# One product per head and direction for the next state and the outputs of an RWKV-7 scan, with the block columns of every second head reversed

## The chip, the cores and the metric

The kernel runs on one core of a Trainium2 chip. The metric is the device time of one execution in microseconds (us); lower is better. The kernel before took 3946.70, 3950.52 and 3961.48 us in three runs, median 3950.52 us.

## What is computed

Two layers of a diffusion backbone on 512 latent and 256 context tokens of 1024 channels in fp32. A layer is a feed-forward, a token mixing, and a second feed-forward. The mixing projects the tokens once, gives half of the channels to a neighbourhood attention and the other half to RWKV-7, a recurrence over tokens that is run forward and backward, and projects both back. Of the recurrence (eight heads of 64 channels) the reference says, per head and direction:

```python
def rwkv_scan(state0, r, decay, k, v, kk, a, reverse):
    emit = r is not None

    def step(S, inp):
        r_t, w_t, k_t, v_t, kk_t, a_t = inp
        removal = jnp.einsum('bhvk,bhk->bhv', S, kk_t)
        S = (S * w_t[:, :, None, :]
             - removal[..., None] * (kk_t * a_t)[:, :, None, :]
             + v_t[..., None] * k_t[:, :, None, :])
        out = jnp.einsum('bhvk,bhk->bhv', S, r_t) if emit else None
        return S, out
```

The context is scanned first, then the latent tokens. In the second (last) layer the context's outputs are not wanted, so `r` is None there.

## The kernel before

Everything is one program; a static scheduler sets the order of the instructions on each engine, and each engine then runs its own list in that order.

**The feed-forwards** (`up`, line 364, and `product`, line 322) are long runs of matrix products with weights split into a high and a low part; they take most of the span and the change does not touch them.

**The mixing** (`mix`, line 1096) issues seven kinds of steps side by side through `drive` (line 71), which hands out the next ready step by weights of TensorE time: the scan (`chains`), the blocks' inverses (`solves`), the blocks (`all_blocks`), the projections, the attention, the modulation of the next layer, and the output projection (`outs`). The scan has the first rank.

**The scan.** The 768 tokens of a direction are cut into 24 chunks of 32. Four heads (two pairs) form a group and are scanned together in both directions, so a chunk has eight head-and-direction products, and there are 2 layers x 2 groups x 24 = 96 chunks. `rwkv_block` (line 780) and `rwkv_solves` (line 746) prepare, for each head, direction and chunk, a block of 128 rows and 128 columns in a tile named `st`. Its columns are `B_S` (64: the next state), `B_O` (32: the outputs), `B_U` (32: U, the removal term of the chunk's tokens). Head e = 0 of a pair keeps the state in rows 0 to 63 and V and U in rows 64 to 127; head e = 1 has it the other way round (`SR`, `VR`, `UR`, line 44).

`rwkv_chain` (line 914) then does, per chunk, on a state tile x (the profile calls it `k`):

- eight products into 32 rows each that give U (line 938), into bank `ch`; ACT copies head 0's part and DVE (line 940) head 1's part back into x;
- eight products into 64 rows each for the next state (line 944), the two heads of a pair in different halves of the rows, into the other half of bank `ch`; ACT and DVE (line 946) copy it into the next state tile;
- where outputs are wanted (80 of the 96 chunks), eight products into 32 rows each (line 950), all into the same 32 rows `QUADS[c]` of bank `co`. After four chunks (a unit) one ACT copy of the whole bank writes the tile `ob`.

After certain units `rwkv_read` (line 987) reads `ob`: a product `pj` (line 996), a chain of small DVE, POOL and ACT steps, transposes (line 1013) and a product `pg` (line 1020). The output projection of these heads follows it.

An fp32 product appears in the trace as two MATMUL records and two LDWEIGHTS records, so eight products are 16 records. "Tile shape" below means the rows and columns of TensorE's array that a product uses, read from the weights' shape: 128\*32, 128\*64, 128\*128 and so on.

Of the kernel before, what the change touches and what calls it, by code (L numbers as in the profile page):

```python
# [12 lines left out]
ALU = mybir.AluOpType  # L13
# [10 lines left out]
# half of the columns of the feed-forward's first product, even as the products ask for  # L24
# [4 lines left out]
# head pairs are scanned two at a time  # L29
# [77 lines left out]
class Net:  # L107
# [62 lines left out]
    def mod(self, l, i, tag, cols, bank):  # L170
# [3 lines left out]
        for c0 in range(0, KD * D, step):  # L174
# [6 lines left out]
            # the four column groups at once  # L181
# [71 lines left out]
    def prep_wino(self, kt, tag="g3"):  # L253
        """The right operands of k-tiles kt and kt + 4: x scaled, and twice the shifts."""
# [51 lines left out]
    def weight(self, src):  # L306
        """The parts of four tiles of weights: (high, low)."""
# [6 lines left out]
    def product(self, w, xh, xl, segs, banks="g"):  # L314
        """The product's segments one after the other: (columns, PSUM) as each is finished."""
# [25 lines left out]
    def up(self, raw, ctx, hh, hl):  # L341
        """A tile of the hidden features."""
# [80 lines left out]
    def accumulate(self, src, k0, n, hh, hl, ctx, gate, after, banks="g"):  # L423
        """Adds the gated product of input tiles k0 to k0 + n to x, two output tiles m and m + 4 at a time."""
# [21 lines left out]
    def head_rms(self, sq, nt, mean, tag, bank):  # L446
        """1/sqrt of each head's sum (or mean) of squares, spread over that head's channels, in PSUM banks."""
# [21 lines left out]
    def qkv(self, l, p, last):  # L469
        """q and k normalised, and v in the order of the windows' key groups, of head pair p, to DRAM."""  # L470
# [31 lines left out]
    def transposed_tiles(self, out, src):  # L502
        """The transposes of six tiles of 128 x 128."""
# [6 lines left out]
    # key groups of v by tokens, of 128: columns 8-23, 24-39, 40-55, 0-7 with 56-63 of all rows, then the context  # L510
    # of each block of 16 query columns: (first column, columns, groups of them, step) of its keys, and their groups of v (group, its first key)
# [268 lines left out]
    def rwkv_block(self, l, p, b, emit, ltd, g):  # L780
# [49 lines left out]
        for h in range(2):  # L830
# [5 lines left out]
            for e, rows in enumerate(SR):  # L836
# [6 lines left out]
                if not emit:  # L843
                    nc.gpsimd.memset(free_ap(st[rows], [[128, 8], [1, 32]], o + 64), 0.0)
# [408 lines left out]
```

## Time and profile before

| | |
|---|---|
| runs before | 3946.70, 3950.52, 3961.48 us (median 3950.52) |
| profiled execution | span 3962.7 us; the profile has no other time of its own |
| PE (matmuls) | 3659.5 us busy, 92% |
| DVE | 2934.9 us, 74% |
| ACT | 1498.9 us, 38% |
| POOL | 1005.3 us, 25% |
| DMA queue | 26.9% of 16 engines |

The page's second part cuts the span in 40 slices of 99 us. Slices 9 to 16 are the mixing of the first layer and slices 29 to 35 that of the second. "Granted clock" is the share of TensorE's full 2.4 GHz that it was given; in the records of a short stretch it is 1.0 (2.4 GHz) or 0.5 (1.2 GHz). In the list of groups, "idle before" is the time for which the engine had nothing to do just before such an instruction, with what ended it. Idle time of an engine that is not the bottleneck costs nothing.

### The profile page before, as it was taken

To read this page: it belongs to the slowest core of one execution; us is meant where nothing else is said; L and a number is where in the kernel's file an instruction comes from. 1 tells how busy PE (TensorE), PEld (TensorE's weight loads), DVE (VectorE), ACT (ScalarE), POOL (GpSimd) and SP (SyncE) were. 2 spreads that over 40 slices of the span, in tenths; PEclk is the share of its full clock that TensorE was granted. 3 is DMA by queue.
4 is the path that set the end of the run, shared out by engine and by line. 5 is a ranking of instruction groups with operands and counts; after the bars stand their busy time and mean duration, and the time that the engine had idled before them with its cause. 6 is when DMAs were issued, how large, how long until landed. Compare 5 with 4: busy or idle time off the path is not lost. (4 is left out here: it accounts for less than half of the span.)

```text
span 3962.7 us, 73554 instructions
## 1 busy us (share of the span) xinstructions
PE 3659.5 (92%) x28980; PEld 3152.3 (80%) x28980; DVE 2934.9 (74%) x5682; ACT 1498.9 (38%) x2968; POOL 1005.3 (25%) x1156
## 2 busy tenths in 40 slices
PE   6999999999799899799999999999998977878988
PEld 4788889878666567699998999998886756768888
DVE  5666678575868766788878888886668686768888
ACT  4232224343444432533335433334434442243333
POOL 2222222020312311322323322230203131133333
PEclk8999999989899779799999999999998885779999
DMA  5333332332245243111121111123322210212222
GB/s 194 123 118 108 107 107 73 102 95 76 69 151 173 90 150 111 66 67 64 65 75 54 65 64 67 66 71 115 108 88 73 68 60 18 70 59 94 82 82 94
DMA packets 229849, 354.62 MB, mean 89 GB/s; under 512 B 47744, under 2 KB 156672, under 8 KB 217216
## 3 DMA queue, kind: packets, MB, share of 16 engines
q1 hardware_dynamic: 229504, 349.92, 26.9%
q8 instruction: 229, 3.75, 0.4%
q14 instruction: 116, 0.95, 0.1%
HBM read 306.31 MB, written 43.52 MB: 88 GB/s over the span
## 5 line engine op out<-in xcount | busy, mean ns | idle before, releaser
L364 PE MATMUL mw<-b,wq 128*128 128x386 f32 (+1 forms) x4224 | 783.4, 329 | 15.5 <-ACT wq L167 9.0
L364 PEld LDWEIGHTS mw<-b,wq 128*128 128x128 f32 x4224 | 701.8, 191 | 40.4 <-ACT wq L167 11.6
L322 PE MATMUL mm<-h,whi 128*128 128x256 f32 (+1 forms) x2816 | 669.9, 331 | 22.1 <-ACT h L167 20.1
L164 DVE SCALAR_TENSOR_TENSOR x<-mm,mods,x 128x256 f32<-128x256 f32 (+1 forms) x768 | 418.0, 573 | 192.8 <-PE mm L322 188.8
L322 PEld LDWEIGHTS mm<-h,whi 128*128 128x128 f32 x2816 | 475.4, 191 | 99.0 <-ACT h L167 23.5
L364 PE MATMUL mw<-b,whi 128*128 128x386 f32 (+1 forms) x2112 | 520.6, 329 | 30.4 <-ACT b L167 11.8
L322 PE MATMUL mm<-h,wlo 128*128 128x256 f32 (+1 forms) x1408 | 450.2, 328 | 2.0 <-DVE wlo L161 1.9
L364 PEld LDWEIGHTS mw<-b,whi 128*128 128x128 f32 x2112 | 373.8, 190 | 40.3 <-ACT b L167 16.0
L167 ACT ACTIVATE whi<-wraw 128x512 fp32r<-128x512 f32 x312 | 196.1, 629 | 493.4 <-PE mm L322 297.1
L364 PE MATMUL mw<-b,wlo 128*128 128x386 f32 (+1 forms) x1056 | 346.6, 328 | 1.1 <-DVE wlo L161 0.8
L167 ACT ACTIVATE wq<-raw 128x512 fp32r<-128x512 f32 x352 | 219.6, 628 | 338.3 <-PE mw L364 264.7
L161 DVE TENSOR_TENSOR wq<-raw,wq 128x512 fp32r<-128x512 f32 x352 | 292.4, 832 | 68.2 <-ACT wq L167 65.3
L322 PEld LDWEIGHTS mm<-h,wlo 128*128 128x128 f32 x1408 | 268.6, 192 | 28.5 <-DVE wlo L161 2.8
L161 DVE TENSOR_TENSOR wlo<-wraw,whi 128x512 fp32r<-128x512 f32 x312 | 222.3, 714 | 54.1 <-ACT whi L167 38.0
L161 DVE TENSOR_TENSOR up_g<-up_g,mw 128x386 f32<-128x386 f32 (+1 forms) x352 | 182.3, 518 | 92.2 <-PE mw L364 75.5
L161 POOL TENSOR_TENSOR raw<-raw,s 128x512 f32<-128x512 f32 x88 | 125.7, 1428 | 432.1 <-DVE wq L161 429.5
L161 POOL TENSOR_TENSOR s<-raw 128x512 f32<-128x512 f32 x88 | 125.2, 1423 | 432.5 <-DVE wlo L161 371.4
L167 ACT ACTIVATE whi<-s 128x512 fp32r<-128x512 f32 x176 | 110.5, 629 | 321.0 <-PE mm L322 229.3
L322 PE MATMUL mm<-x,whi 128*128 128x258 f32 (+2 forms) x832 | 207.5, 335 | 0.0
L364 PEld LDWEIGHTS mw<-b,wlo 128*128 128x128 f32 x1056 | 201.1, 190 | 3.2 <-DVE wlo L161 2.4
L184 PE MATMUL modps<-wmod,cs 128*32 128x256 f32 x1152 | 172.7, 427 | 23.6 <-DMA wmod<-in_w_mod_dram 22.9
L161 POOL TENSOR_TENSOR up_g<-up_g,rstd 128x386 f32<-128x386 f32 (+1 forms) x88 | 103.5, 1176 | 342.8 <-DVE up_g L161 337.9
(226 smaller groups left out, 7043.5 us busy)
## 6 DMA issues: line engine op xcount, KB each, us to landing
raw<-in_ffn_up_dram SPq DMA_DIRECT2D x88, 1024.0 KB, 5.4
wraw<-in_ffn_down_dram SPq DMA_DIRECT2D x176, 256.0 KB, 3.1
wmod<-in_w_mod_dram SPq DMA_DIRECT2D x144, 256.0 KB, 3.1
wmod<-in_w_mod_dram SPq DMA_DIRECT2D x224, 128.0 KB, 2.2
wraw<-in_w_in_dram SPq DMA_DIRECT2D x104, 256.0 KB, 2.8
wmod<-in_w_mod_dram SPq DMA_DIRECT2D x8, 1024.0 KB, 10.9
wraw<-in_w_out_dram SPq DMA_DIRECT2D x32, 256.0 KB, 3.1
in<-rkv SPq DMA_DIRECT2D x20, 384.0 KB, 3.9
```

Of the source, the lines that this page charges most:

```text
L161: (eng or self.nc.vector).tensor_tensor(out=out, in0=a, in1=b, op=op)
L164: self.nc.vector.scalar_tensor_tensor(out=out, in0=a, scalar=s, in1=b, op0=op0, op1=op1)
L167: self.nc.scalar.activation(out, in_, f, **kw)
L184: nc.tensor.matmul(ps[q:q + 32], lhsT=self.cs[:, kt], rhs=w, start=kt == 0, stop=kt == KD - 1)
L322: nc.tensor.matmul(ps, lhsT=wt, rhs=xt[k][:, c0:c1], start=k == 0 and n == 0, stop=k == nk - 1 and n == 2)
L364: nc.tensor.matmul(ps, lhsT=wt[:, c], rhs=self.bs[i][k][xt], start=k == 0 and m == 0, stop=k == 3 and m == 2)
```

## The change

The columns of head 1's blocks are reversed in order: U, outputs, state. Since head 1's state belongs in rows 64 to 127 of the bank, its state and outputs then stand in the right rows if all 128 columns are used as weights, and head 0's if its first 96 columns are. One product per head and direction (line 953 of the new kernel) gives both, into a bank `so` per chunk. The U products are as before (line 942). The outputs are copied to `ob` after each chunk, by two ACT copies of 32 rows, in place of one copy of 128 rows after four chunks. Where no outputs are wanted, the product has the 64 state columns alone.

```diff
-B_S, B_O, B_U, SW = slice(0, 64), slice(64, 96), slice(96, 128), 2048
+B_S, B_O, B_U, SW = (slice(0, 64), slice(64, 128)), (slice(64, 96), slice(32, 64)), (slice(96, 128), slice(0, 32)), 2048
+
+B_SO, B_OU = (slice(0, 96), slice(32, 128)), (slice(64, 128), slice(0, 64))
...
             if emit:
-                po = self.bank("co", "co", (128, 2, 4, 64))
+                obs[u] = self.t("ob", "ob").rearrange("p (e n v) -> p e n v", e=2, n=4)
             for c in range(4):
...
-                ps = self.bank("ch", "ch", (128, 2, 4, 64))
+                ps = self.bank("ch", "ch", (128, 4, 64))
...
+                so = self.bank("co", "so", (128, 2, 4, 64))
+                for y, d, n in heads:
+                    for e, rows in enumerate(SR):
+                        if emit:
+                            cols, rows = (slice(0, 96), slice(0, 96)) if e == 0 else (slice(0, 128), slice(0, 128))
+                        else:
+                            cols = B_S[e]
+                        nc.tensor.matmul(so[rows, e, n], lhsT=bl(y, e, d, c)[:, cols], rhs=x[:, e, n], start=True, stop=True)
                 if j < 23:
-                    for y, d, n in heads:
-                        for e, rows in enumerate(SR):
-                            nc.tensor.matmul(ps[rows, 1, n], lhsT=bl(y, e, d, c)[:, B_S], rhs=x[:, e, n], start=True, stop=True)
-                    self.act(x2[SR[0], 0], ps[SR[0], 1], AF.Copy)
-                    nc.vector.tensor_copy(x2[SR[1], 1], ps[SR[1], 1])
+                    self.act(x2[SR[0], 0], so[SR[0], 0], AF.Copy)
+                    nc.vector.tensor_copy(x2[SR[1], 1], so[SR[1], 1])
                 if emit:
-                    for y, d, n in heads:
-                        for e in range(2):
-                            nc.tensor.matmul(po[QUADS[c], e, n], lhsT=bl(y, e, d, c)[:, B_O], rhs=x[:, e, n], start=True, stop=True)
+                    for e in range(2):
+                        self.act(obs[u][QUADS[c], e], so[B_O[e], e], AF.Copy)
                 yield E["c"]
-            if emit:
-                obs[u] = self.t("ob", "ob").rearrange("p (e n v) -> p e n v", e=2, n=4)
-                self.act(obs[u], po, AF.Copy)
```

Elsewhere in the diff the same operations address the moved columns (`B_S[e]`, `B_O[e]`, `B_U[e]`); their number and shapes stay.

In numbers of instructions, counted in the two programs: on PE 736 products of 64 rows and 640 of 32 rows go, and 320 of 96 rows, 320 of 128 rows and 128 of 64 rows come. On ACT 20 copies of 128x512 go and 160 of 32x256 come, and there are two more loads of a function table (51 become 53). DVE, POOL and the DMA queue issue as many instructions as before. From one PE product to the next the tile shape changes 1451 times before and 1344 times now. The scheduler lays the whole mixing out anew. Between the state products and the next chunk's U products there is no other work on PE in 1 place before and in 8 now, and between the U products and the state products in 3 places before and in 9 now.

Three places on PE (`mm` is the output projection, `o` its operand).

One chunk of the second layer's last unit, before:

```order
L938 MATMUL ch<-k_26202,st 32x64 x8
L322 MATMUL mm<-o_33855,whi 128x256
...
L322 MATMUL mm<-o_33861,wlo 128x256
L950 MATMUL co<-k_26202,st 32x64
L944 MATMUL ch<-k_26202,st 64x64 x8
L950 MATMUL co<-k_26202,st 32x64 x7
L322 MATMUL mm<-o_33855,whi 128x256
```

and the same unit's last chunk now:

```order
L942 MATMUL ch<-k_25954,st 32x64 x8
L325 MATMUL mm<-o_33501,whi 128x256
...
L325 MATMUL mm<-o_33507,wlo 128x256
L953 MATMUL so<-k_25954,st 96x64
L953 MATMUL so<-k_25954,st 128x64
L953 MATMUL so<-k_25954,st 96x64
L953 MATMUL so<-k_25954,st 128x64
L953 MATMUL so<-k_25954,st 96x64
L953 MATMUL so<-k_25954,st 128x64
```

The three bursts `co`, `ch`, `co` have become one burst `so`, which alternates between 96 and 128 rows.

An earlier stretch of the same group, where the next unit's products (`gt`, `bops`) are mixed in, before:

```order
L950 MATMUL co<-k_26202,st 32x64
L944 MATMUL ch<-k_26202,st 64x64 x8
L950 MATMUL co<-k_26202,st 32x64 x7
L856 MATMUL gt<-st,bk 64x128 x8
L714 MATMUL bops<-ts,consts 128x512
L938 MATMUL ch<-k_26202,st 32x64 x8
L714 MATMUL bops<-ts,consts 128x512
L950 MATMUL co<-k_26202,st 32x64
L944 MATMUL ch<-k_26202,st 64x64 x8
L950 MATMUL co<-k_26202,st 32x64 x7
L938 MATMUL ch<-k_26203,st 32x64 x8
```

and now:

```order
L717 MATMUL bops<-ts,consts 128x512
L942 MATMUL ch<-k_25954,st 32x64 x8
L717 MATMUL bops<-ts,consts 128x512
L953 MATMUL so<-k_25954,st 96x64
...
L953 MATMUL so<-k_25954,st 128x64
L942 MATMUL ch<-k_25955,st 32x64 x8
```

Seven output products stood between the state products and the next U products; now nothing stands there.

The end of the first layer's scan, from its last output products to the transposes of the first of its two last readouts, before:

```order
L950 MATMUL co<-k_6100,st 32x64 x7
L1020 MATMUL pg<-sg,gg 128x128 x2
L322 MATMUL mm<-o_15020,whi 128x512
...
L322 MATMUL mm<-o_15026,wlo 128x256
L996 MATMUL pj<-ob,consts 128x256
L322 MATMUL mm<-o_15020,whi 128x512
...
L322 MATMUL mm<-o_15026,wlo 128x256
L1013 MATMUL pt_15768<-consts,o 128x128 x2
```

and now, with the second readout too:

```order
L953 MATMUL so<-k_6100,st 128x64
L1002 MATMUL pj<-ob,consts 128x256
L1019 MATMUL pt_15520<-consts,o 128x128 x2
L1026 MATMUL pg<-sg,gg 128x128 x2
L1002 MATMUL pj<-ob,consts 128x256
L1019 MATMUL pt_15552<-consts,o 128x128 x2
```

The 48 `mm` products that stood behind the last output products (12 ahead of `pj`, 36 behind it) have moved to earlier places.

## Rows read from the trace of the kernel before

**Rows 1.** The page: engines' busy time, and the granted clock in 40 slices.

```profile
PE 3659.5 (92%) x28980; PEld 3152.3 (80%) x28980; DVE 2934.9 (74%) x5682; ACT 1498.9 (38%) x2968; POOL 1005.3 (25%) x1156
PEclk8999999989899779799999999999998885779999
```

**Rows 2.** Three stretches of the scan: busy us by engine (records), granted clock, DMA.

```profile
860.00:1000.00 140.00, 136.32 (x1396) 115.04 (x1395) 81.51 (x161) 53.75 (x101) 19.09 (x36) 0.96 0.28 85
1130.00:1575.00 445.00, 422.50 (x5271) 294.46 (x5267) 316.72 (x752) 176.85 (x425) 93.06 (x166) 0.89 0.44 138
...
3100.00:3495.00 395.00, 331.27 (x4397) 266.91 (x4395) 282.58 (x640) 141.21 (x331) 85.58 (x157) 0.77 0.18 56
```

**Rows 3.** The page: the chain that ended last, by line.

```profile
PE mm L322 5%; PE mw L364 3%; DMA raw<-in_ffn_up_dram 1%; PE ap L759 1%; DVE st L161 1%; DVE wlo L161 1%; DVE wq L161 1%; DVE pr L161 1%; PE ch L938 1%; PE co L950 1%; PE gt L856 1%; PE ch L944 1%; DVE x L164 1%; DVE up_u L161 0%; PE px L905 0%
```

**Rows 4.** PE's groups of the scan: busy us, mean ns, idle before, what ended it.

```profile
L950 PE MATMUL co<-k,st 128*32 128x64 f32 x1280 | 115.7, 233 | 5.7 <-ACT k L167 4.8 <-DVE k L940 0.9
...
L944 PE MATMUL ch<-k,st 128*64 128x64 f32 x1472 | 85.2, 248 | 23.1 <-DVE k L940 21.4 <-ACT st L167 1.4 <-DVE st L764 0.3
L938 PE MATMUL ch<-k,st 128*32 128x64 f32 (+1 forms) x1536 | 76.5, 241 | 16.1 <-DVE k L946 16.1
```

**Rows 5.** Weight loads and products by line: min/median/max ns, first and last start, shapes.

```profile
L950 PEld LDWEIGHTS co<-k,st x1280: 106/110/178, 899.8 to 3494.9; 128*32 128x32 f32 x183
L950 PE MATMUL co<-k,st x1280: 219/219/317, 899.8 to 3495.0; 128*32 128x64 f32 x183
```

```profile
L944 PEld LDWEIGHTS ch<-k,st x1472: 132/138/232, 899.5 to 3488.8; 128*64 128x64 f32 x184
```

```profile
L451 PEld LDWEIGHTS hss<-consts,sqh x176: 186/192/195, 781.3 to 3008.9; 128*128 128x128 f32 x176
```

**Rows 6.** PE in order of time, one chunk at full clock: start us, length us.

```profile
3467.53 0.64 PE L938 MATMUL ch<-k,st 96*32 96x64 f32 x16
...
3469.50 0.28 PE L322 MATMUL mm<-o,wlo 128*128 128x256 f32 x1
3469.71 0.30 PE L950 MATMUL co<-k,st 128*32 128x64 f32 x2
3469.94 0.69 PE L944 MATMUL ch<-k,st 128*64 128x64 f32 x16
3470.55 0.97 PE L950 MATMUL co<-k,st 128*32 128x64 f32 x14
3471.45 0.51 PE L322 MATMUL mm<-o,whi 128*128 128x256 f32 x2
...
3473.49 0.58 PE L938 MATMUL ch<-k,st 96*32 96x64 f32 x14
```

**Rows 7.** PE in order of time, full-width weights with two moving columns.

```profile
2964.24 0.61 PE L451 MATMUL hss<-consts,sqh 128*128 128x2 f32 x4
...
2965.39 0.83 PE L451 MATMUL hss<-consts,sqh 128*128 128x2 f32 x6
```

**Rows 8.** ACT's groups: the scan's copies and the table loads.

```profile
L167 ACT ACTIVATE k<-ch 32x256 f32<-32x256 f32 (+1 forms) x188 | 70.7, 376 | 207.3 <-PE ch L938 124.2 <-PE ch L944 75.1 <-DVE st L161 2.3
L167 ACT ACT_TABLE_LOAD x50 | 64.2, 1283 | 0.9
...
L167 ACT ACTIVATE ob<-co 128x512 f32<-128x512 f32 x20 | 11.9, 593 | 12.5 <-PE co L950 12.5
```

**Rows 9.** DVE's copy of the next state: min/median/max ns.

```profile
L946 DVE COPY k<-ch x92: 420/427/429, 907.8 to 3489.9; 64x256 f32<-64x256 f32 x92
```

**Rows 10.** PE at the end of the first layer's scan, in order of time.

```profile
1578.84 0.60 PE L996 MATMUL pj<-ob,consts 128*128 128x256 f32 x2
...
1586.37 0.27 PE L1013 MATMUL pt<-consts,o 128*128 128x128 f32 x1
```

**Rows 11.** PE at the end of the second layer's scan, in order of time.

```profile
3496.23 0.70 PE L996 MATMUL pj<-ob,consts 128*128 128x256 f32 x2
3501.41 0.47 PE L1013 MATMUL pt<-consts,o 128*128 128x128 f32 x1 [4.48 <-POOL o L161]
```

More of the change, by code (lines that the diff above doesn't have):

```diff
@@ L759, in rwkv_solves @@
                                 nc.tensor.matmul(ps[UR[e], c], lhsT=ti[UR[e], 16 * y + 8 * d + 4 * (u % 2) + c],
-                                                 rhs=self.block(g["stage"][y, u], e, d, c)[UR[e], 0:96], start=True, stop=True)
+                                                 rhs=self.block(g["stage"][y, u], e, d, c)[UR[e], B_SO[e]], start=True, stop=True)
                         for e in range(2):
-                            dst = self.blocks(g["stage"][y, u], e, d)[UR[e], :, 0:96]
+                            dst = self.blocks(g["stage"][y, u], e, d)[UR[e], :, B_SO[e]]
                             if e:
@@ L836, in rwkv_block @@
             for e, rows in enumerate(SR):
-                o = 1024 * e
+                o = 1024 * e + B_S[e].start
                 one = self.consts[rows, C_ID + 64 * e:C_ID + 64 * e + 64]
@@ L843, in rwkv_block @@
                 if not emit:
-                    nc.gpsimd.memset(free_ap(st[rows], [[128, 8], [1, 32]], o + 64), 0.0)
+                    nc.gpsimd.memset(free_ap(st[rows], [[128, 8], [1, 32]], 1024 * e + B_O[e].start), 0.0)
                 for d in range(2):
@@ L848, in rwkv_block @@
                     bl = self.blocks(st, e, d)[rows].rearrange("p (s h) m -> p s h m", h=2)
-                    self.tt(bl[:, :, :, B_U], c4(order(kk[d][rows, now], d)), pq[:, :, 0:64].rearrange("p s (h t) -> p s h t", h=2), ALU.mult, self.nc.gpsimd)
+                    self.tt(bl[:, :, :, B_U[e]], c4(order(kk[d][rows, now], d)), pq[:, :, 0:64].rearrange("p s (h t) -> p s h t", h=2), ALU.mult, self.nc.gpsimd)
                     if emit:
-                        self.tt(bl[:, :, :, B_O], c4(order(r[d][rows, now], d)), pq[:, :, 1:65].rearrange("p s (h t) -> p s h t", h=2), ALU.mult)
+                        self.tt(bl[:, :, :, B_O[e]], c4(order(r[d][rows, now], d)), pq[:, :, 1:65].rearrange("p s (h t) -> p s h t", h=2), ALU.mult)
             for d in range(2):
@@ L860, in rwkv_block @@
                     bl = self.blocks(st, e, d)
-                    self.act(bl[o, :, B_S], gt[o, :, B_S], AF.Copy)
-                    self.tt(bl[o, :, 64:128], gt[o, :, 64:128], free_ap(self.c(C_MG)[o], [[0, 4], [1, 64]]), ALU.mult)
+                    self.act(bl[o, :, B_S[e]], gt[o, :, B_S[e]], AF.Copy)
+                    halves = lambda t: t[o, :, B_OU[e]].rearrange("p c (a m) -> p c a m", a=2)
+                    self.tt(halves(bl), halves(gt), free_ap(self.c(C_MG)[o], [[0, 4], [32 - 64 * e, 2], [1, 32]], 32 * e), ALU.mult)
                     n = 16 * y + 8 * d + 4 * h
-                    nc.vector.tensor_scalar(ltd[UR[e], n:n + 4], bl[UR[e], :, B_U], 1.0, None, ALU.mult)
+                    nc.vector.tensor_scalar(ltd[UR[e], n:n + 4], bl[UR[e], :, B_U[e]], 1.0, None, ALU.mult)
             yield E["b"]
@@ L910, in rwkv_solve @@
             for u in (2 * b, 2 * b + 1):
-                nc.gpsimd.memset(free_ap(g["stage"][y, u][UR[1]], [[128, 8], [1, 32]], 1024 + 96), 0.0)
+                nc.gpsimd.memset(free_ap(g["stage"][y, u][UR[1]], [[128, 8], [1, 32]], 1024 + B_U[1].start), 0.0)
         return tt
@@ L934, in rwkv_chain @@
                 x, x2 = self.xs[j % 4], self.xs[(j + 1) % 4]
-                ps = self.bank("ch", "ch", (128, 2, 4, 64))
+                ps = self.bank("ch", "ch", (128, 4, 64))
                 for y, d, n in heads:
                     for e, k in enumerate((slice(0, 96), slice(0, 128))):
-                        nc.tensor.matmul(ps[UR[e], 0, n], lhsT=bl(y, e, d, c)[k, B_U], rhs=x[k, e, n], start=True, stop=True)
-                self.act(x[UR[0], 0], ps[UR[0], 0], AF.Copy)
-                nc.vector.tensor_copy(x[UR[1], 1], ps[UR[1], 0])
@@ L941, in rwkv_chain @@
-                if j < 23:
-                    for y, d, n in heads:
-                        for e, rows in enumerate(SR):
-                            nc.tensor.matmul(ps[rows, 1, n], lhsT=bl(y, e, d, c)[:, B_S], rhs=x[:, e, n], start=True, stop=True)
-                    self.act(x2[SR[0], 0], ps[SR[0], 1], AF.Copy)
-                    nc.vector.tensor_copy(x2[SR[1], 1], ps[SR[1], 1])
+                        nc.tensor.matmul(ps[UR[e], n], lhsT=bl(y, e, d, c)[k, B_U[e]], rhs=x[k, e, n], start=True, stop=True)
@@ new lines, in rwkv_chain @@
+                self.act(x[UR[0], 0], ps[UR[0]], AF.Copy)
+                nc.vector.tensor_copy(x[UR[1], 1], ps[UR[1]])
+                so = self.bank("co", "so", (128, 2, 4, 64))
[6 more added lines that the diff above has]
+                        nc.tensor.matmul(so[rows, e, n], lhsT=bl(y, e, d, c)[:, cols], rhs=x[:, e, n], start=True, stop=True)
```

2 lines of the change are left out of this document (1 added, 1 removed).

## Prediction

> **What bounds the kernel now.** The page's first part is read first: PE is busy for 3659.5 of 3962.7 us [rows 1]. ACT has 38%, so a copy more or less on ACT counts only where something waits for it. The change touches the scan alone, so the stretches of the scan come next [rows 2]. In the first layer PE is busy for 136.3 of 140 and 422.5 of 445 us: there the end is set by PE's work, and each microsecond added to it or taken from it moves the end. In the second layer it is busy for 331.3 of 395 us at a mean granted clock of 0.77: there PE waits in turns for DVE, ACT and the scan, and the clock falls to its lower level of 1.2 GHz in between. The chain that ended last has all three scan lines on it, U (line 938), state (line 944) and outputs (line 950), at 1% of the span each [rows 3]: some 120 us in all, about 80 of them on the two that change. Last, PE's groups: outputs 115.7 us busy, state 85.2, U 76.5, with 5.7, 23.1 and 16.1 us of idle time before them [rows 4].
>
> **The products.** One chunk with outputs at full clock is read from the timeline [rows 6]. A record lasts 0.22 us [rows 5], so the starts of the 14 output records in 0.97 us span 0.97 - 0.22 = 0.75 us, 0.058 a step; 16 records take 16 x 0.058 = 0.92 us. The 16 state records take 0.69 us, so their starts span 0.47 us: seven steps of a pair, nearly as short as one step of the outputs. The two heads of a pair go to different columns of the array and run side by side; the outputs of all heads go to the same 32 columns and can't. With one more pair step (0.06) the state burst is 0.53 us, and both together 1.45 us.
>
> The new products use columns 0 to 95 and 0 to 127, so none can run beside another. No row has weights of 96 columns and 64 moving ones. The nearest with full width is `hss`, with two moving columns: six records take 0.83 us and four 0.61 us, so a step is 0.11 us though hardly anything moves [rows 7]. The step there is the load's. A load lasts 110, 138 and 192 ns for 32, 64 and 128 columns [rows 5], 0.84 ns per column from 64 to 128, so a load of 96 is 27 ns shorter than one of 128, and I take 0.085 us for its step. A burst is then 8 x (0.11 + 0.085) = 1.56 us, and 0.05 at its start, by which the state burst's 0.47 us exceeds seven steps of 0.06: 1.61 us. That is 0.16 us more than before. It counts in 76 chunks, 12.2 us; the last chunk of each of the four groups had outputs alone (0.92 us) and pays 0.69 us more, 2.8 us. Together +15.0 us at full clock. The bounds: a 96-column record at the outputs' 0.058 makes the burst 1.39 us (-0.06 a chunk, -2.7 us in all); at the full 0.11 it makes 1.81 us (+0.36, +31 us). I take the value between by the slope, as the load rows are nearest.
>
> **The changes of tile shape.** The last of 14 output records starts 0.75 us after 3470.55, the next product (another shape) at 3471.45: 0.15 us, where a step is 0.06 [rows 6]. A change of shape costs 0.09 us. There are 1451 before and 1344 now, so -107 x 0.09 = -9.6 us. Products and shapes make +5.4 us at full clock; over a granted clock of about 0.87 (the three stretches' mean, by their length nearer to 0.85) [rows 2] that is **+6 us**, and by the bounds -14 to +25.
>
> **The copies without cover.** Seven output products stood between the state products and the next U products while ACT and DVE copied the state. There are now 7 places more with no other work on PE between state and U, and 6 more between U and state. In each PE waits for the end of the last record (0.22) and DVE's copy (0.43) [rows 5, 9]: 13 x 0.65 = **+8.5 us**; at least 0, if PE would have waited anyway, and 17 if the copies come late as often again.
>
> **The end of the first layer's scan.** The 48 output-projection products behind its last chunk are now used up earlier. Between `pj` and `pt` of its first late readout PE had 7.5 us of them [rows 10]; the same readout in the second layer, with nothing beside it, shows 4.48 us of waiting for POOL [rows 11]. **+4.5 us**, from 0 (the products saved as many waits where they now stand) to 9 (both readouts). The second layer's end was bare before and stays so.
>
> **ACT.** 160 copies of about 0.376 us for 20 of 0.593, and two table loads of 1.28 [rows 8]: 60.2 - 11.9 + 2.6 = +51 us. They lie beside PE's work on an engine that is 38% busy. Only where the two output copies (0.75 us) stand ahead of ACT's next U copy can they be seen, and there the U burst itself lasts 0.64 us [rows 6], which hides all but 0.1: at most 8 us in 80 chunks. I take **+3 us**, with 0 and 15 as ends (whatever else ACT delays). The bank `so` must be empty before the next chunk's products; its copies stand in ACT's list ahead of the next U copy, so nothing waits for that alone. The 5.7 us that PE stood idle before output products [rows 4] go: **-5.7 us**.
>
> DVE, POOL and the DMA queue keep their counts and sizes; the smaller U bank and the reversed columns cost nothing, as the same instructions address other columns.
>
> **The sum.** 6 + 8.5 + 4.5 + 3 - 5.7 = +16.3 us. The profiled execution's span is 3962.7 us, 12.2 above the median of the runs shown and 1.2 above the slowest; it would become 3979.0. Against the median of 3950.5 that is 3966.8, **3967 us** (+0.41%). About 0.5%, 19.8 us, is what a measurement of this kernel can tell from no change, so this is within it, not far from the edge.
>
> **Rivals.**
>
> *The width is free.* If a record costs what its 64 moving columns cost, 0.058 us however wide the weights are, the burst is 0.93 + 0.05 = 0.98 us, 0.47 less in 76 chunks: -36 us, with the shapes -45, over 0.87 -52; with the other terms -42: 3909 us (-1.1%). For it: the outputs' step matches the moving columns and not their load. Against it: `hss` [rows 7], 0.11 us a step with two moving columns. It decides when a pair of new records takes less than about 0.14 us. Chance 0.11. The Trainium skill (TensorEngine Tiling, Performance Considerations, Instruction Overhead) says that each matmul has about 60 cycles of overhead and that one with a free dimension of 1 is as slow as one of 60; it names no cost of wider weights, and so by that rule this rival is what happens. The trace speaks against it where the weights are 128 wide, with the 0.11 us of `hss`.
>
> *96 columns cost as much as 128.* Then +25 in place of +6: 3986 us (+0.9%). For it: both use the same shape of array; against it the slope of the loads. Chance 0.10.
>
> *The scan becomes the bound of the second layer.* Each of its 32 chunks with outputs gets its next state only after the whole burst, 1.61 - 0.53 = 1.08 us later, 1.4 at a clock of 0.77, and with ACT's 0.1 about 1.5 us: +48 us in place of the uncovered copies there, with the rest about 4005 us (+1.4%). For it: 37.5 us of idle time already end on DVE's copies [rows 4]. Against it: a chunk starts every 5.96 us [rows 6], and its two bursts and two copies add up to 2.1 us (0.64, 0.38, 0.69, 0.43); the scan has slack until its chunks take over 6. Chance 0.12.
>
> *Nothing of it shows.* The products moved forward fill waits as long as those they leave, and the work lands in idle time of the second layer: 3940 to 3958. Chance 0.17. *The new order wins time elsewhere*, over 20 us, for no reason in the rows: 0.08, at about 3925.
>
> **The chances.** The forecast, from 3955 to 3985 us, has 0.42, of which 0.25 lies within 0.5% and 0.17 above. Faster: 0.11 + 0.08 = 0.19. Same: 0.25 + 0.17 = 0.42. Slower: 0.17 + 0.10 + 0.12 = 0.39. The range from 3922 to 4010 leaves out the free width and the far end of the scan as bound.
>
> **What would show it.** Bursts of 16 `so` records at full clock from first to last start in about 1.5 us, steps of 0.11 and 0.085 in turn, none side by side; loads of about 165 ns for 96 columns. No 0.09 us around `so` where output-projection products stand next to it. Idle time before U ended by DVE's `k` copy up from 16.1 us. A bare wait of 4 to 5 us before `pt` at the end of the first layer's scan. ACT some 50 us busier. The prediction is wrong if a pair of `so` records takes under 0.14 or over 0.22 us, or if the second layer's scan moves by over 20 us.

## The result, and the profile after

The changed kernel takes 4060.16 us (median of four runs, 4043.34 to 4072.31) against 3952.80 us for the kernel before: a ratio of 1.0259, 95% interval 1.0232 to 1.0285. It is slower, by 107 us, and outside the range of the prediction. The four runs themselves go with the granted clock: 4043.34 us had a mean of 0.914, 4072.31 us, the profiled one, 0.904.

The page of the changed kernel, its first part and its row of the clock [rows 1]:

```profile
PE 3749.8 (92%) x27764; PEld 3232.4 (79%) x27764; DVE 2939.5 (72%) x5682; ACT 1551.7 (38%) x3110; POOL 1006.5 (25%) x1156
PEclk7999999899877778799999999999998775779999
```

PE is busy for 90 us more with 1216 records fewer, and the slices of the two mixings (9 to 16 and 29 to 35) hold more sevens. The view of spans and clocks, of the kernel before and then after, says how much that is:

```profile
core 0: 3962.7 us, clock 0.926
```

```profile
core 0: 4070.5 us, clock 0.904
```

Span times clock is the length at full clock, span times (1 - clock) is what the lower level of 1.2 GHz took. Before: 3669 and 293 us. After: 3680 and 391 us. **Of the 108 us of this pair, 98 are the clock and 10 are all else.** The time at 1.2 GHz, twice the second number, goes from 587 to some 783 us (the records of the clock add up to 785). Over all executions whose span and clock are on record (61 of the kernel before, taken beside the runs below, and four of the changed one) the means are 3674 and 282 us before, 3687 and 370 after: 88 of 101 us are the clock. The 98 count half of all time at 1.2 GHz as lost, idle time too. Splitting PE's busy time by level is stricter: work at full clock goes from 3427 to 3432 us, what this work loses at 1.2 GHz from 233 to 318, idle time from 303 to 321.

The windows of the scan [rows 2]; the second and third stretch lie later now, by what the kernel had lost until there. Behind its length a line has the busy us and records of PE, of its weight loads, DVE, ACT and POOL, then the granted clock, the DMA share and GB/s:

```profile
860.00:1000.00 140.00, 135.56 (x1271) 117.86 (x1269) 82.08 (x159) 59.66 (x116) 18.35 (x37) 0.94 0.29 85
1150.00:1590.00 440.00, 407.26 (x4073) 286.46 (x4071) 266.02 (x638) 167.73 (x414) 83.78 (x149) 0.76 0.38 117
3190.00:3595.00 405.00, 352.81 (x3850) 287.01 (x3846) 276.89 (x627) 160.25 (x377) 82.81 (x155) 0.71 0.17 52
```

The first is as before (0.96, now 0.94). The clock of the second fell from 0.89 to 0.76, that of the third from 0.77 to 0.71. By the trace's `mw` records, the first layer's mixing (from the last record of the feed-forward ahead of it to the first of the one behind) lasts 1070 us where it lasted 997, and the second layer's 906 where it lasted 879: 73 and 27 us. In the first, 62 of the 73 are lost at 1.2 GHz.

The groups of the scan on PE [rows 4], and the merged product's loads and records [rows 5]:

```profile
L953 PE MATMUL so<-k,st 128*96 128x64 f32 (+2 forms) x1536 | 212.6, 300 | 26.8 <-DVE k L944 15.1 <-ACT k L170 10.2 <-ACT ob L170 0.9
...
L942 PE MATMUL ch<-k,st 96*32 96x64 f32 (+1 forms) x1536 | 99.4, 255 | 17.8 <-DVE k L956 10.4 <-ACT k L170 5.3 <-POOL st L915 1.8
```

```profile
L953 PEld LDWEIGHTS so<-k,st x1536: 132/192/338, 898.5 to 3599.4; 128*96 128x96 f32 x160, 128*64 128x64 f32 x32
L953 PE MATMUL so<-k,st x1536: 217/275/476, 898.6 to 3599.4; 128*96 128x64 f32 x160, 128*64 128x64 f32 x32
```

PE in order of time at the last chunk of the second layer [rows 6, 11]:

```profile
3598.01 1.71 PE L953 MATMUL so<-k,st 128*96 128x64 f32 x16
...
3607.34 0.48 PE L1019 MATMUL pt<-consts,o 128*128 128x128 f32 x1 [4.11 <-POOL o L164]
```

and at the end of the first layer's scan [rows 10]:

```profile
1654.30 0.70 PE L1002 MATMUL pj<-ob,consts 128*128 128x256 f32 x2 [0.85 <-ACT ob L170]
1659.11 0.48 PE L1019 MATMUL pt<-consts,o 128*128 128x128 f32 x1 [4.11 <-POOL o L164]
...
1666.53 0.47 PE L1019 MATMUL pt<-consts,o 128*128 128x128 f32 x1 [4.11 <-POOL o L164]
```

ACT's groups [rows 8]:

```profile
L170 ACT ACTIVATE ob<-so 32x256 f32<-32x256 f32 x160 | 59.9, 374 | 75.2 <-DVE k L956 64.0 <-PE so L953 5.4 <-PE pj L1002 4.3
...
L170 ACT ACTIVATE k<-so 64x256 f32<-64x256 f32 x92 | 34.6, 376 | 132.8 <-PE so L953 132.6
```

DVE's copy of the state lasts 428 ns in the median, as before (427) [rows 9].

One wait is new. State and outputs of a chunk now lie in one PSUM bank, and its readers go one after the other: ACT's copy of the state, DVE's, ACT's two output copies. ACT stands 64.0 us in its own list until DVE has made its copy, where before it waited only for PE, 12.5 us [rows 8]. The Trainium skill (PSUM — Partial Sum Buffer, section PSUM bank collisions raise a hardware error) says that reads of one bank by two engines collide in the same 32 partitions, so that a program has to keep them apart. The new wait agrees with that for the first output copy, which reads rows 64 to 95 while DVE reads rows 64 to 127; the second (rows 32 to 63) merely stands behind it in ACT's list.

### The profile page after: what moved, and what is told of

It is laid out like the page before. It is cut to its first block, busy times and chain, and to the rows that moved or that the text cites. A ratio compares the mean times of both kernels' runs of the same rounds, so it can differ in the third digit from the quotient of the medians.

```text
span 4070.5 us, 71303 instructions
## 1 busy us (share of the span) xinstructions
PE 3749.8 (92%) x27764; PEld 3232.4 (79%) x27764; DVE 2939.5 (72%) x5682; ACT 1551.7 (38%) x3110; POOL 1006.5 (25%) x1156
## 5 line engine op out<-in xcount | busy, mean ns | idle before, releaser
L953 PEld LDWEIGHTS so<-k,st 128*96 128x96 f32 (+2 forms) x1536 | 191.6, 210 | 64.4 <-DVE k L944 17.8
L953 PE MATMUL so<-k,st 128*96 128x64 f32 (+2 forms) x1536 | 212.6, 300 | 26.8 <-DVE k L944 15.1
## 6 DMA issues: line engine op xcount, KB each, us to landing
wmod<-in_w_mod_dram SPq DMA_DIRECT2D x8, 1024.0 KB, 10.4
```

The lines of the kernel that those rows point to most:

```text
L953: nc.tensor.matmul(so[rows, e, n], lhsT=bl(y, e, d, c)[:, cols], rhs=x[:, e, n], start=True, stop=True)
```

## The experiments

Theories: **A**, ACT's list is held by the output copies in the shared bank. **B**, an output tile is now taken at a unit's start and the scan stands for want of one. **C**, the re-laid order is an accident. **D**, the longer burst makes the next state late and slows the scan. **E**, the wide products cost PE's time or clock wherever they stand. **F**, the loss is the granted clock, and depends on what PE does in the shadow of the state's copies, where the separate output products lay. Times are medians with ratio to the kernel before and 95% interval; the kernel before was at 3957 to 3960 us beside them. Span and clock are the profiled execution's, and the two columns behind them are worked out from these. "All executions" has the means of the same two numbers over all executions of the run (4 to 10; 61 of the kernel before). One execution is a small sample: where the two differ, as in runs 9 and 13, the means are the better evidence. "Mixings" are the lengths of the first and the second layer's mixing in the profiled trace, as above. ("Half-clock time" is the time at 1.2 GHz.)

| run | time, us | ratio | span, clock | at full clock | lost at 1.2 GHz | all executions: full clock, lost | mixings, us |
|---|---|---|---|---|---|---|---|
| before | 3952.8 | | 3962.7, 0.926 | 3669 | 293 | 3674, 282 | 997, 879 |
| after | 4060.2 | 1.0259 (1.0232 to 1.0285) | 4070.5, 0.904 | 3680 | 391 | 3687, 370 | 1070, 906 |
| 1 early tile | 3962.0 | 1.0021 (1.0004 to 1.0038) | 3960.8, 0.930 | 3684 | 277 | 3676, 286 | 996, 878 |
| 2 copies per chunk | 3942.2 | 0.9963 (0.9950 to 0.9977) | 3943.7, 0.933 | 3679 | 264 | 3682, 260 | 987, 863 |
| 3 outputs by DVE | 4029.6 | 1.0171 (1.0126 to 1.0216) | 4040.2, 0.912 | 3685 | 356 | 3686, 337 | 1032, 915 |
| 4 layout alone | 3960.9 | 1.0010 (0.9993 to 1.0027) | 3956.7, 0.927 | 3668 | 289 | 3674, 285 | 1000, 871 |
| 5 wide state products | 4083.8 | 1.0320 (1.0289 to 1.0351) | 4083.1, 0.918 | 3748 | 335 | 3753, 330 | 1073, 920 |
| 6 separate, one bank | 3966.0 | 1.0021 (1.0005 to 1.0036) | 3965.6, 0.924 | 3664 | 301 | 3668, 296 | 1003, 879 |
| 7 two banks | 4007.9 | 1.0120 (1.0087 to 1.0153) | 4012.1, 0.914 | 3667 | 345 | 3672, 335 | 1037, 884 |
| 8 other weight | 4056.8 | 1.0243 (1.0204 to 1.0282) | 4049.1, 0.908 | 3677 | 373 | 3681, 372 | 1047, 914 |
| 9 outputs first | 3993.2 | 1.0090 (1.0060 to 1.0120) | 3998.3, 0.912 | 3646 | 352 | 3665, 328 | 1004, 905 |
| 10 by parity | 4046.9 | 1.0210 (1.0184 to 1.0236) | 4051.6, 0.911 | 3691 | 361 | 3695, 348 | 1029, 926 |
| 11 two banks, parity | 4020.8 | 1.0164 (1.0121 to 1.0208) | 4010.8, 0.921 | 3694 | 317 | 3697, 328 | 1019, 898 |
| 12 before by parity | 3985.1 | 1.0066 (1.0045 to 1.0087) | 3982.9, 0.933 | 3716 | 267 | 3711, 274 | 1003, 891 |
| 13 few outputs | 3958.2 | 1.0003 (0.9985 to 1.0021) | 3943.1, 0.921 | 3632 | 312 | 3628, 328 | 995, 864 |
| 14 long filling | 4029.3 | 1.0186 (1.0152 to 1.0220) | 4024.9, 0.930 | 3743 | 282 | 3755, 273 | 1034, 902 |
| 15 short filling | 4168.2 | 1.0527 (1.0499 to 1.0555) | 4166.6, 0.899 | 3746 | 421 | 3751, 413 | 1120, 958 |
| 16 filling, separate | 4014.2 | 1.0147 (1.0114 to 1.0180) | 4000.8, 0.939 | 3757 | 244 | 3748, 265 | 1007, 901 |

**1. The output tile at the unit's start, in the kernel before.**

```diff
             if emit:
                 po = self.bank("co", "co", (128, 2, 4, 64))
+                obs[u] = self.t("ob", "ob").rearrange(...)
...
-                obs[u] = self.t("ob", "ob").rearrange(...)
                 self.act(obs[u], po, AF.Copy)
```

> The kernel before, with only the output tile of a unit taken at the unit's start (as the change does) and not after its fourth chunk; products and copies as before. Theory A (ScalarE's queue is held by the new output copies, which wait for VectorE's copy out of the same PSUM bank): no effect, 3953 us within 0.5%. Theory B (an output tile is held a unit longer, and with four tiles the scan stands at a unit's start until older units are read out): most of the loss is here, 4000 to 4060 us, and the gaps at the unit starts of the first layer's second group (about 30 us each in the profile of after) show. Theory C (any change of the program re-lays the scheduled order, and the loss is an accident of that): some time that has nothing to do with the wait, 3940 to 4060 us.

+0.2%: B falls.

**2. Output copies per chunk, in the kernel before.**

```diff
-                po = self.bank("co", "co", (128, 2, 4, 64))
+                obs[u] = self.t("ob", "ob").rearrange(...)
...
                 if emit:
+                    po = self.bank("co", "co", (128, 2, 4, 64))
...
+                    for e in range(2):
+                        self.act(obs[u][QUADS[c], e], po[QUADS[c], e], AF.Copy)
```

> The kernel before with its separate state and output products, but the outputs in a bank per chunk and copied by ScalarE in two copies per chunk into the output tile taken at the unit's start, as the change does. The output copies here wait for TensorE alone, since state and outputs lie in different banks. Theory A: only the copies' own time, at most +15 us over the run with the early tile: 3953 to 3970 us. Theory B: as the run with the early tile, 4000 to 4060 us, plus at most 15. If the 160 added copies in themselves cost the time: 4010 to 4060 us here and 3953 in the run with the early tile.

The 160 copies on ACT and the early tile cost nothing; this run is even 0.4% faster than the kernel before, below A's range, at the same length at full clock within 10 us and with some 20 to 30 us less lost at 1.2 GHz. It is the only version that beats both kernels.

**3. The output copies on DVE, in the changed kernel.**

```diff
-                        self.act(obs[u][QUADS[c], e], so[B_O[e], e], AF.Copy)
+                        nc.vector.tensor_copy(obs[u][QUADS[c], e], so[B_O[e], e])
```

> The changed kernel with the two output copies of a chunk on VectorE instead of ScalarE, behind VectorE's own copy of the state: ScalarE no longer waits for VectorE there, VectorE gets 160 copies of 32x256 (some 60 us of work). Theory A: most of the 107 us comes back, 3960 to 3990 us. Theory B: stays, 4030 to 4080 us. If the merged products in the shared bank are what costs (the next chunk's product waits for the copies): stays too, 4040 to 4080 us.

31 of the 107 us come back, and the lost time at 1.2 GHz falls by 35: A has a part, not the whole.

**4. The reversed columns alone.** `B_S[e]`, `B_O[e]` and `B_U[e]`, with the products, banks and copies of before.

```diff
-    lhsT=bl(y, e, d, c)[:, B_S], rhs=x[:, e, n]
+    lhsT=bl(y, e, d, c)[:, B_S[e]], rhs=x[:, e, n]
```

> The kernel before with the blocks' columns of every second head reversed (U, outputs, state instead of state, outputs, U) and all products, banks and copies as before: same shapes, same number of instructions. Theories A and B: 3953 us within 0.3%. Theory C, or a cost of the layout itself in the preparation: more than 15 us away from 3953.

As all expected but C: the layout is free.

**5. Wide state products, separate outputs.** Run 4 with 96 and 128 columns in the state products. Both heads' rows then meet in one place of the bank and the second overwrites the first one's state.

```diff
-    ps[rows, 1, n], lhsT=bl(y, e, d, c)[:, B_S[e]]
+    k = slice(0, 96) if e == 0 else slice(0, 128)
+    ps[k, 1, n], lhsT=bl(y, e, d, c)[:, k]
```

> The kernel with reversed columns and all banks and copies as before, but the state products take 96 and 128 columns instead of 64, as the merged ones do; the output rows they make are thrown away, and the separate output products stay (TensorE does the outputs twice). The state's copies wait for a burst of 1.6 us instead of 0.7. Theory A (the loss sits in the copies out of the shared bank: ScalarE, VectorE and ScalarE again read it one after the other, each waiting for the one before): only TensorE's added work, about 0.9 us for each of 92 chunks at the clock of 0.87, at most +95 if all were bare, some +20 to +60 by the share of the PE-bound stretches; no longer waits for output copies. Theory D (the longer burst between U and the next state is what slows the scan): about +70 to +110, 4030 to 4060 us. Theory E (the price of the wide products is as read, and a bound TensorE pays it): +80, and clock as before (0.92).

+124 us: 79 at full clock, the added work (92 x 0.9 = 83), and 42 by the clock. It shows the price of the width as predicted. It is above D's range and above E's +80, so D and E are not told apart by it.

**6. Separate products in the shared bank**, in the changed kernel.

```diff
-                        if emit:
-                            cols, rows = (slice(0, 96), slice(0, 96)) if e == 0 else (slice(0, 128), slice(0, 128))
-                        else:
-                            cols = B_S[e]
-                        nc.tensor.matmul(so[rows, e, n], lhsT=bl(y, e, d, c)[:, cols], ...)
+                        nc.tensor.matmul(so[rows, e, n], lhsT=bl(y, e, d, c)[:, B_S[e]], ...)
...
                     nc.vector.tensor_copy(x2[SR[1], 1], so[SR[1], 1])
                 if emit:
+                    for y, d, n in heads:
+                        for e in range(2):
+                            nc.tensor.matmul(so[B_O[e], e, n], lhsT=bl(y, e, d, c)[:, B_O[e]], ...)
```

> The changed kernel with its banks and copies, but separate state and output products again (state products, the state's copies, output products into the same bank, output copies). Theory A: the loss stays in the main, 4010 to 4060 us. Theory D: back to 3945 to 3970 us. Theory C (an accident of the scheduled order): anything between 3945 and 4060.

3966 us: banks, copies and the early tile of the change together cost 0.2%. ACT's wait before its output copies is as long, but for PE:

```profile
L170 ACT ACTIVATE ob<-so 32x256 f32<-32x256 f32 x160 | 59.9, 374 | 90.4 <-PE so L957 83.2 <-PE pj L1002 5.2 <-DVE mods L164 0.2
```

A's range is missed and D's is met. So the loss comes with the merging itself.

**7. Two banks.** First heads' half in bank `co`, second heads' in the free half of `ch`; ACT copies the one, DVE the other.

```diff
-                so = self.bank("co", "so", (128, 2, 4, 64))
+                so = [self.bank("co", "so", (128, 4, 64)), ps[:, 1]]
...
-                    for e in range(2):
-                        self.act(obs[u][QUADS[c], e], so[B_O[e], e], AF.Copy)
+                    self.act(obs[u][QUADS[c], 0], so[0][B_O[0]], AF.Copy)
+                    nc.vector.tensor_copy(obs[u][QUADS[c], 1], so[1][B_O[1]])
```

> The changed kernel with the merged product's two halves in two banks (every first head in the bank of the outputs, every second in the unused half of U's bank); ScalarE copies state and outputs of the first heads, VectorE of the second ones, so that neither waits for the other there. Theory A: the loss goes, 3940 to 3980 us. Theory D: it stays, 4030 to 4070 us. Theory C: anything between.

4008 us, between A and D, which is C's range too: half the loss goes with the copies' waits for each other (and with half of the output copies moved to DVE).

**8. Another weight in the issue order.**

```diff
-c=(0.1, 5.5)
+c=(0.1, 7.0)
```

> The changed kernel, with the scan's weight in the table of the issue order set from (0.1, 5.5) to (0.1, 7.0): the same instructions in another order. Theories A and D: 4060 us within 20. Theory C: over 25 us away from 4060, to either side.

3.4 us from the changed kernel: this re-laying doesn't move it. C falls as far as one such change tells. All runs together tell more: but for runs 1 and 4, which keep the order of the kernel before on PE nearly throughout, each has an order of its own. The kernel before and the six runs with separate products of the old widths and all outputs (1, 2, 4, 6, 9, 12) lie from 3942 to 3993 us, the changed kernel and the five runs with merged products and no filling (3, 7, 8, 10, 11) from 4008 to 4060.

**9. Outputs ahead of the state.** Run 6 with the eight output products moved ahead of the eight state products.

```diff
                 so = self.bank("co", "so", (128, 2, 4, 64))
+                if emit:
+                    for y, d, n in heads:
+                        for e in range(2):
+                            nc.tensor.matmul(so[B_O[e], e, n], lhsT=bl(y, e, d, c)[:, B_O[e]], ...)
                 if j < 23:
...
                 if emit:
-                    for y, d, n in heads:
-                        for e in range(2):
-                            nc.tensor.matmul(so[B_O[e], e, n], lhsT=bl(y, e, d, c)[:, B_O[e]], ...)
```

> The run with separate products in one bank (3966 us), with the eight output products of a chunk put ahead of its eight state products instead of behind the state's copies: the same instructions, the same shapes and the same work of TensorE, but a chunk's next state is finished about 0.74 us later, as with the merged product. Theory D (the scan's chain from chunk to chunk sets the pace of the mixing, and the longer burst ahead of the state's copies is what costs): most of the loss comes back, 4030 to 4070 us. Theory E (the widths and shapes of the merged products cost TensorE's time or clock, wherever they stand): 3966 us within 15.

+27 us over run 6, far from the 64 at least that D wanted and past E's 15. Over the ten executions of each, the length at full clock differs by 3 us and 32 more are lost at 1.2 GHz (the profiled pair has -18 and +51). The late state, or the empty shadow of its copies, counts, and it counts by the clock. In the traces all of it lies in the second layer's mixing, 879 us in run 6 and 905 here; the first layer's is 1003 and 1004. The changed kernel has 906 in the second and 1070 in the first. So the second layer's part of its loss comes without merged products too, and the 67 us that are left for these lie in the first layer.

**10 to 12. The order by head parity**, in the changed kernel, in run 7 and in the kernel before.

```diff
-                for y, d, n in heads:
-                    for e, ... in enumerate(...):
+                for e, ... in enumerate(...):
+                    for y, d, n in heads:
```

> The changed kernel with the products of U and of the merged burst ordered by head parity, four products of the first heads and then four of the second ones, instead of alternating: ScalarE's copy of the first heads can start after half of the burst (0.7 to 0.8 us sooner), and shapes change twice per chunk and burst instead of eight times. Theory D: a good part of the loss goes, 3980 to 4035 us. Theory E by the changes of shape alone: some 0.09 us for each of about 7 changes less in 92 bursts, 60 us, about 4000 us; then the steps of the products in the trace must fall below 85 and 112 ns. Neither: 4060 us within 15.

> The run with the two halves in two banks (4008 us) with the same order by head parity. Theory D: the chain is shorter again (neither copy waits for the other, and the first starts half a burst sooner), 3940 to 3990 us. Theory E: as in the run by head parity alone, less the 50 us of the split.

> The kernel before, with the products of U and of the state ordered by head parity; output products as before. Same instructions. Theory D: ScalarE's copies start about 0.35 us sooner in both steps of a chunk and VectorE's, which wait for them in the same bank, as much: up to 0.7 us in each of some 70 chunks that set the pace, 3905 to 3945 us. Theory E: 3953 us, or up to 10 less.

All three missed D's numbers; run 12 is slower where D wanted it faster, and outside E's range too. Run 10 is where neither theory holds: its steps are 85 and 112 ns as before. PE in order of time, in run 12:

```profile
3484.79 0.89 PE L938 MATMUL ch<-k,st 96*32 96x64 f32 x16
...
3487.66 0.97 PE L944 MATMUL ch<-k,st 128*64 128x64 f32 x16
```

The bursts take 0.89 and 0.97 us where they took 0.64 and 0.69 [rows 6]: the two heads of a pair run side by side when they stand next to each other, which the prediction had read off and these expectations forgot. 0.53 us in 92 chunks is 49 us, and the length at full clock grows by 47 in the profiled pair, by 38 over all executions. Whether a sooner first copy is worth something is not told apart by these runs, as it was bought with longer bursts.

**13. Few outputs.** The kernel before, without the output products of three chunks in four, and the fourth's with 128 columns; the outputs of three chunks in four are not computed.

```diff
-                if emit:
+                if emit and c == 3:
...
-   po[QUADS[c], e, n], lhsT=bl(y, e, d, c)[:, B_O]
+   po[:, e, n], lhsT=bl(y, e, d, c)
```

> The kernel before, with the output products of three of each four chunks left out (and those of the fourth made 128 columns wide, so that the unit's bank is written in full): 24 short products per unit go, some 40 us of TensorE's work, nothing is merged and the chain from chunk to chunk is as it was. Its outputs are in part not computed. Theory F (the merged kernel loses by the granted clock: without the separate output products in the copies' shadow, TensorE stands at 1.2 GHz longer): time at half clock in the profile goes up by 80 us or more from the 587 us of the kernel before, and the time stays at 3940 to 4000 us in spite of less work. Theory D or plain work: 3905 to 3920 us, half-clock time within 50 us of 587.

960 records fewer, 37 us less at full clock, and the median did not move: 3958 against 3957 us. F's time holds. By the profile, which F names, its size doesn't: the time at 1.2 GHz grows from 587 to 621 us, by 34 and not 80. But the profiled execution was the fastest of ten. Over all ten, against the 13 of the kernel before beside them, the length at full clock falls by 47 us and the lost time grows by 48, which is 96 us more at 1.2 GHz: all that the work saved goes back by the clock.

**14 to 16. Products that nobody reads, in the shadow of the state's copies**: ahead of a chunk's U products: two of 256 columns in the changed kernel (14), four of 64 (15), and two of 256 in run 6 (16). The edit of run 14, and then the product of run 15:

```diff
+                for n in range(2):
+                    nc.tensor.matmul(ps[:, 1], lhsT=self.c(0), rhs=self.c(0, 256), start=True, stop=True)
```

```diff
+                for n in range(4):
+                    nc.tensor.matmul(ps[:, 1, n], lhsT=self.c(0), rhs=self.c(0, 64), start=True, stop=True)
```

> The changed kernel with two added products of 128 rows x 256 columns on the constants per chunk, into an unused part of U's bank, that land in the shadow of the state's copies: about 2 x 0.43 us x 96 = 80 us more work for TensorE, nothing reads them. Theory F: the half-clock time falls from 786 us by 150 or more, and the time is 4000 to 4075 us, not slower than the changed kernel in spite of the work. If work is work and the clock does not answer: 4110 to 4150 us.

> As the run with long added products, but with four products of 128x64 per chunk (0.22 us each by the steps of the merged ones, so the same 0.9 us per chunk). If all that counts for the clock is that TensorE is not left without work during the copies, the result is as with the long ones; if short products do nothing for the clock: 4110 to 4150 us, half-clock time near 786 us or more.

> The run with separate products in one bank (3966 us) with the same two long products added per chunk. Theory F: half-clock time falls from its 603 us by 100 or more and takes back half to all of the added 80 us of work: 3955 to 4010 us. If the clock does not answer: 4040 to 4055 us.

Two long products more per chunk make the changed kernel 31 us **faster**, though its length at full clock grows: by 68 us over all executions, with 97 less lost at 1.2 GHz (63 and 109 in the profiled pair). F holds here. The same added time in short products makes it 108 us slower, with 64 us more at full clock and 43 more lost; this is 18 us above the range that was named for short products that do nothing. In run 16 the long ones win back 31 of the 80 us that they cost; 48 us are left, above F's upper end by 4. The added products stand where they were meant to in most places: 85 of their 98 groups in run 14, and 86 of 101 in run 15, directly follow a merged burst. The added products' groups in runs 14 and 15 are equal in busy time:

```profile
L941 PE MATMUL ch<-consts 128*128 128x256 f32 x384 | 126.4, 459 | 4.4 <-DMA consts<-in_consts_dram 3.7 <-DVE k L946 0.7
```

```profile
L941 PE MATMUL ch<-consts 128*128 128x64 f32 x768 | 128.1, 320 | 3.7 <-DMA consts<-in_consts_dram 3.7
```

The window from 1150 to 1250 us, the first 100 us of the loss, of the kernel before, of the changed kernel, and of runs 14 and 15:

```profile
1150.00:1250.00 100.00, 99.92 (x1396) 67.21 (x1396) 74.95 (x192) 46.03 (x121) 20.65 (x42) 1.00 0.55 172
```

```profile
1150.00:1250.00 100.00, 97.63 (x1012) 71.14 (x1009) 50.18 (x130) 38.89 (x101) 20.70 (x37) 0.74 0.34 103
```

```profile
1150.00:1250.00 100.00, 99.19 (x1121) 68.77 (x1117) 57.13 (x145) 41.87 (x111) 16.47 (x33) 0.91 0.37 114
```

```profile
1150.00:1250.00 100.00, 100.00 (x993) 71.65 (x991) 38.42 (x99) 33.21 (x87) 10.38 (x22) 0.72 0.27 82
```

PE is busy for practically the whole window in all four, and did 1396, 1012, 1121 and 993 records in it. What goes with it is the clock: 1.00, 0.74, 0.91, 0.72.

## Why the prediction was wrong

**The step that failed** is "over a granted clock of about 0.87". The clock was read from the kernel before and used as a constant factor on the added work; what the change does to the clock had no term. It is 98 of the 108 us of the profiled pair, and 88 of 101 over all executions. The rest of the sum, +16.3 us by the prediction, is 10 or 13 us by the lengths at full clock.

**The products** were priced well. In stretches of full clock the records of the merged burst start 112 and 85 ns apart (medians of over 150 steps of each kind), as forecast from `hss` and the slope of the loads; 96-column loads take 165 ns (median of some 440 at full clock). The last burst's 16 records take 1.71 us, less the last one's 0.22 gives 1.49 from first to last start, as forecast. Where an `mm` product stands next to the burst, the step is 118 ns ahead of it and 84 behind it (medians), without the 0.09 us of a change of shape, as forecast. Work at full clock grew by 5 us, forecast 5.4. The rival that the width is free fell: 128 columns of weights cost twice the 0.058 us of 32. The rule of the Trainium skill (TensorEngine Tiling, Performance Considerations, Instruction Overhead) named there gives no cost of the width, so it does not forecast these steps.

**The copies without cover** were forecast at +8.5 us and the outputs' idle time at -5.7. The idle time before the scan's products was 44.9 us [rows 4] and is 17.8 + 26.8 = 44.6: both small, their sum near nothing. The waits before U that end on DVE's copy fell from 16.1 to 10.4 us instead of rising. Their price isn't in idle time.

**The end of the first layer's scan**: the bare wait for POOL is there, 4.11 us, in two readouts. Right, at the far end of its range.

**ACT** got 52.8 us busier, forecast 51. That "nothing waits for that alone" held for PE, which waited 0.9 us for the output copies. What the prediction left out is that these copies wait for DVE in ACT's list, 64.0 us in 54 places, and all behind them waits too. Runs 3 and 7 give back 31 and 52 us with that wait gone, most of it at 1.2 GHz, so this is part of what brought the clock down. It does not do so alone. Run 9 has the wait at 3993 us, and run 14 has more of it with less lost at 1.2 GHz than the changed kernel; the group in run 9 and in run 14:

```profile
L170 ACT ACTIVATE ob<-so 32x256 f32<-32x256 f32 x160 | 59.9, 375 | 72.0 <-DVE k L957 67.8 <-PE so L950 2.5
```

```profile
L170 ACT ACTIVATE ob<-so 32x256 f32<-32x256 f32 x160 | 59.9, 374 | 82.6 <-DVE k L958 76.4 <-PE so L955 3.4 <-PE pj L1004 1.5
```

**The rival of the scan as the second layer's bound** named 4005 us and a mechanism (the next state comes after the whole burst). The prediction's own sign for it, a second layer's scan that moves by over 20 us, came true with 27, and run 9 has the same 27 there with separate products. But 73 us of the loss lie in the first layer, where the prediction said that PE's work sets the end and had nothing but this work to add. The work grew there by little; 62 of the 73 us are work and waits at 1.2 GHz.

**What is shown and what is not.** Shown: the loss is time at 1.2 GHz (the lengths at full clock), most of it needs the merged products (run 6 against the change), a quarter of it comes with outputs ahead of the state in separate products (run 9), and work put behind the merged burst takes the lost time back if it is long products (14) and not if it is short ones of the same duration (15). Not shown: why the clock answers to the one and not to the other, whether long products would do the same elsewhere, whether in run 9 it is the late state or the empty shadow that counts, and how the rest divides between the merged products and the waits of the copies for each other.

## What to carry to other kernels

Before a change to TensorE's stream is priced, split the span into its length at full clock and what is lost at 1.2 GHz, and ask what the change does to the second; here it was 88 of 101 us, and the prediction had the first right within 6. Take that split from several executions: in runs 9 and 13 the lost time of the profiled one alone was 24 and 16 us off their means. A cut in the number of small products is not a gain in itself: taking 1216 records out of the stream left TensorE's work the same and the clock lower. And when outputs move into a bank that another engine reads, look who waits for whom in the list of the engine that copies them.

## What the runs showed that was not expected

- A stretch in which TensorE is busy without a gap can run at 1.2 GHz for more than half of its time: 100.00 of 100 us at a mean granted clock of 0.72 (run 15).
- Useless work can pay: 384 records of 256 columns nobody reads, 126.4 us busy, and the kernel is 31 us faster than without them (run 14).
- ScalarE's 160 small copies beside the scan cost nothing (run 2), and where their bank was their own, the kernel was 0.4% faster than with 20 large ones.
